# SBUF start addresses of matmul operands, first loads on a second queue, output pieces laid crosswise, row sums taken on VectorE

## The chip, the core and the metric

The kernel runs on one core of a Trainium2 chip. The number that counts is the time of one execution in device microseconds (us). Five engines work side by side, each on its own instructions in their order: TensorE (PE in the rows; its weight loads are PEld), VectorE (DVE), ScalarE (ACT), GpSimd (POOL) and SyncE (SP), which issues most of the DMAs. They wait for each other by semaphores.

## What is computed

One decoder layer over 256 tokens of width 1024, in float32, with five mixer branches that read the same input x. Cut to what matters:

```
h = x @ w_in + b_in                     # 1024 -> about 14000 columns: q, k, v, gates z, merge logits
o_a = causal attention                  # branch A
o_b = dilated mixture:                  # branch B: three (q, k) groups, one v
      parts = [band(q_i, k_i, v, window, dilation) for the 3 groups]
      num/den merged over the groups    # = one softmax over the three groups' logits
o_c, o_d, o_e = forgetting attention, gated delta rule, memory cross-attention
o = stack(o_a .. o_e) * silu(z)
y = sum_n sigmoid(merge_logits_n) * (o_n @ w_branch_n)
y = y @ w_out
out = layer_norm(alpha * x + y) * ln_g + ln_b
```

## The kernel before

**Matmuls.** Every float32 operand of a large matmul is split into a high part (`hi`) and the rest (`lo`), both stored in a 4-byte matmul format: ScalarE writes `hi` by a copy (L123), VectorE writes `lo = src - hi` (L124). A product then takes three matmuls, `hi*hi`, `hi*lo`, `lo*hi` (`mm3`, L128). So weights are loaded to `raw` (4 KB a partition), split into `hi` and `lo`, and used from there. x is split once, into `xhi` and `xlo`.

**Units.** The work on weights is a list of units in the order `ORDER`. A projection unit (`fm_unit`) has 1024 weight columns, which is 24 matmuls with the 256 columns of x moving and 128 weight columns stationary; in the rows it reads `mm<-xhi,hi`, `mm<-xlo,hi`, `mm<-xhi,lo` (moving operand first). A merge of a branch (`merge_branch`) has eight pairs: one such unit for the merge logits, then a unit of nine matmuls in which the gated branch output moves (`mm<-f,hi`, `mm<-f,lo`). There are 40 pairs. The memory's keys take three units with `big` (the normalised memory) moving. A token-major block (`tm_block`) has the weights moving and x stationary; the first block of all is one of these, on `wcs` (402 columns, 48 matmuls). The last stage is y @ w_out: 120 matmuls with weights moving (512 or 256 columns) and `f` stationary, in five pieces.

**Order.** Units come one after the other; between their chunks, `stepper` emits the next step of side streams (attention of branches a, b, c, the delta rule, the memory's layer norm, cross-attention). A timeline scheduler then orders instructions on each engine, apart from those that `keep` pins to the order of the program. Loads run up to four units ahead, in five `raw` buffers (`NRAW`): SP issues a load when VectorE has made the `lo` part of the unit that used the buffer.

**Placing.** Tiles of a partition lie behind each other in the order in which the pools were opened. By the built program `xhi` and `xlo` start at bytes 16512 and 24704 (both 128 past a multiple of 512), the five `raw`, four `hi` and four `lo` buffers from byte 62144 on in steps of 4096 (all 192 past one), the sixteen `f3` buffers, where gated outputs and y lie, from 115392 on in steps of 3072 (192 past one), the `big` buffers from 164544 on (192 past one). Chunks of a tile that a matmul takes are 512 or 1024 bytes apart, so each keeps its tile's remainder.

**Start.** x comes in five pieces, two of 128 KB and three of 256 KB, between the four loads of `wcs`, all from SP; the pieces of x lie in two `raw` buffers.

**Branch b.** `attend` (L752 to L790) handles two heads at a time (a pair, x = 0, 1), three pairs. Per head: logits with mask and row minimum on VectorE (L752), exponentials on ScalarE (L768) for three groups with `accum_out`, which adds the row sums; VectorE adds group 1, then group 2, to group 0 (L771), adds the three row sums (L775), takes the reciprocal and scales (L781). TensorE transposes the result (L787).

**Tail.** `finish` computes block t of 128 tokens piece by piece into PSUM tiles of two banks. Both halves of block 0 lie in one tile, both of block 1 in the other. Each piece is read by VectorE (L1071), which adds the residual; statistics, reciprocal root and two VectorE instructions per half (L1062, L1063) follow, then the store.

Of the kernel before, what the change touches and what calls it, by code (L numbers as in the profile page):

```python
# [9 lines left out]
F32 = mybir.dt.float32  # L10
# [5 lines left out]
P = 128  # L16
S = 256
# [58 lines left out]
@with_exitstack  # L76
def kernel(ctx: ExitStack, tc: tile.TileContext, T: dict, out: bass.AP):
    nc = tc.nc
    cpool = ctx.enter_context(tc.tile_pool(name="cpool", bufs=1))
    wpool = ctx.enter_context(tc.tile_pool(name="wpool", bufs=3))  # L80
    f3 = ctx.enter_context(tc.tile_pool(name="f3", bufs=16))
    big = ctx.enter_context(tc.tile_pool(name="big", bufs=2))
    sp = ctx.enter_context(tc.tile_pool(name="sp", bufs=4))
    ps = ctx.enter_context(tc.tile_pool(name="ps", bufs=2, space=bass.MemoryType.PSUM))
    dr = ctx.enter_context(tc.tile_pool(name="dr", bufs=1, space=bass.MemoryType.DRAM))
# [33 lines left out]
        return pst("av", shape, 1)  # L119


    def split(hi, lo, src):
        A_.activation(hi, src, AF.Copy)  # L123
        V_.tensor_tensor(lo, src, hi.bitcast(F32), op=ALU.subtract)  # L124

    def mm3(pt, lh, ll, rh, rl, first, last, pin=False):
# [10 lines left out]
    HR = (slice(0, 64), slice(64, 128))  # L137


    xhi, xlo = ct("xhi", (P, KD, S), F32R), ct("xlo", (P, KD, S), F32R)  # L140
    cst = ct("cst", (P, C_N))
    vb, vcb = ct("vb", (P, 2, BW)), ct("vcb", (P, BW + 18))
    bcol = ct("bcol", (P, T["bcol"].shape[1]))
# [19 lines left out]
    class Unit:  # L163
# [7 lines left out]
        def load(self):  # L171
            self.r = wpool.tile([P, 1024], F32, tag="raw", name=nm("raw"), bufs=NRAW)
            for i, p in enumerate(self.parts):
                if self.before is not None:
                    self.before[0](i, len(self.parts))
                nc.sync.dma_start(self.r[:, p], self.src[:, p])

        def split(self):
            self.h = wpool.tile([P, 1024], F32R, tag="hi", name=nm("hi"), bufs=NHI)
            self.l = wpool.tile([P, 1024], F32R, tag="lo", name=nm("lo"), bufs=NHI)  # L180
            for i, p in enumerate(self.parts):
                if self.before is not None:
                    self.before[1](i, len(self.parts))
                split(self.h[:, p], self.l[:, p], self.r[:, p])

    def need(name):
        while name is not None and name not in done:
# [88 lines left out]
    xraw = {}  # L276

    def load_x(i, j, n):
        if i % 2 == 0 and j == 0:
            xraw["t"] = wpool.tile([P, 4, S], F32, tag="raw", name=nm("raw"), bufs=NRAW)  # L280
        w = 2 // n
        o = 2 * i + w * j
        xraw[i, j] = xraw["t"][:, o % 4:o % 4 + w]
        nc.sync.dma_start(xraw[i, j], T["xT"][:, o:o + w])

    def split_x(i, j, n):
        w = 2 // n
        o = 2 * i + w * j
        split(xhi[:, o:o + w], xlo[:, o:o + w], xraw[i, j])

    def evac_c(p, t):
        if t == 0:
# [10 lines left out]
    def consts():  # L303
        for _ in range(CW):
            yield 1
        nc.sync.dma_start(vcb, T["vcb"].to_broadcast([P, BW + 18]))
        nc.sync.dma_start(bcol, T["bcol"])
        nc.sync.dma_start(cw, T["convw"])
        nc.sync.dma_start(adt, T["adt"].to_broadcast([P, 12]))
        nc.sync.dma_start(cst[:, :C_MA], T["cst"][:, :C_MA])  # L310
        flag("consts")


# [6 lines left out]
    def scalars():  # L320

        yield from wait("sc")
        nc.sync.dma_start(cst[:, C_MA:], T["cst"][:, C_MA:])
        nc.sync.dma_start(gnw, T["gnw"])
        nc.sync.dma_start(mgb, T["mgb"])
        nc.sync.dma_start(vb, T["vb"].to_broadcast([P, 2, BW]))

        V_.tensor_scalar(cwh, cw, 0.5, None, op0=ALU.mult)
        hb = bcol[:, 3 * len(FM):]
        V_.tensor_scalar(hb, hb, 0.5, None, op0=ALU.mult)  # L330
        for n, f in [("z" + i, 0.5) for i in BR] + list(QSCALE.items()):
            i = FM.index(n) * 3
            V_.tensor_scalar(bcol[:, i:i + 3], bcol[:, i:i + 3], f, None, op0=ALU.mult)
        flag("bias")
        yield
        a, lp = ct("a", (P, 2, 12)), ct("lp", (P, 2, 12))
        e, s1, s2, ea = ct("e", (P, 24)), ct("s1", (P, 24)), ct("s2", (P, 24)), ct("ea", (P, 6))
        for t in range(2):
            V_.tensor_scalar(a[:, t, 0:6], sc[:, t, 0:6], -1.0, None, op0=ALU.mult)
            V_.tensor_tensor(a[:, t, 6:12], sc[:, t, 6:12], adt[:, 6:12], op=ALU.add)  # L340
        af, lpf = a.rearrange("p t c -> p (t c)"), lp.rearrange("p t c -> p (t c)")
        V_.scalar_tensor_tensor(e, af, -1.0, af, op0=ALU.mult, op1=ALU.max)
        A_.activation(beta, sc[:, :, 12:18], AF.Exp, scale=-1.0)
        A_.activation(ea, adt[:, 0:6], AF.Exp)
        yield
        A_.activation(e, e, AF.Exp, scale=-1.0)
        V_.tensor_scalar(beta, beta, 1.0, None, op0=ALU.add)
        V_.reciprocal(beta, beta)
        V_.tensor_scalar(ea, ea, -1.0, None, op0=ALU.mult)
        yield  # L350
        V_.tensor_scalar(s1, e, 2.0, None, op0=ALU.add)
        V_.reciprocal(s1, s1)
        V_.tensor_tensor(s1, s1, e, op=ALU.mult)
        V_.tensor_tensor(s2, s1, s1, op=ALU.mult)
        V_.tensor_scalar(lpf, s2, 2.0 / 17, None, op0=ALU.mult)
        for n in (15, 13, 11, 9, 7, 5, 3):
            V_.scalar_tensor_tensor(lpf, lpf, 2.0 / n, s2, op0=ALU.add, op1=ALU.mult)
        V_.scalar_tensor_tensor(lpf, lpf, 2.0, s1, op0=ALU.add, op1=ALU.mult)
        V_.scalar_tensor_tensor(lpf, af, 0.0, lpf, op0=ALU.max, op1=ALU.add)
        yield  # L360

        for t in range(2):
            V_.tensor_scalar(fg[:, t, 0:6], lp[:, t, 0:6], -1.0, None, op0=ALU.mult)
            V_.tensor_tensor(lp[:, t, 6:12], lp[:, t, 6:12], ea, op=ALU.mult)
            V_.tensor_scalar(fg[:, t, 6:12], lp[:, t, 6:12], MAGIC, -MAGIC, op0=ALU.add, op1=ALU.add)
            V_.tensor_tensor(fg[:, t, 12:18], lp[:, t, 6:12], fg[:, t, 6:12], op=ALU.subtract)
        yield BURST

        lg = lgps()
        pt, p2 = lg[:, 0, :36].rearrange("p (t c) -> p t c", t=2), lg[0:18, 1, :S]  # L370
        keep(PE.matmul(pt[:, 0], K(C_TRI), fg[:, 0], start=True, stop=True))
        keep(PE.matmul(pt[:, 1], K(C_ONE), fg[:, 0], start=True, stop=False))
        keep(PE.matmul(pt[:, 1], K(C_TRI), fg[:, 1], start=False, stop=True))
        keep(PE.matmul(p2, fg[:, 0], K(C_TRI, 256), start=True, stop=False))
        keep(PE.matmul(p2[:, P:], fg[:, 1], K(C_TRI), start=False, stop=True))
        yield
        V_.tensor_scalar(ngt, pt, -1.0, None, op0=ALU.mult)
        grow = ct("grow", (18, S))
        V_.tensor_copy(grow, p2)
        R["gscr"] = dr.tile([18, S], F32, name="gscr")  # L380
        yield
        nc.sync.dma_start(R["gscr"], grow)
        flag("scalars")
# [340 lines left out]
    def attend(br, groups, vname, maskf, width):  # L724
# [5 lines left out]
        def pair(m):  # L730
# [33 lines left out]
            for g in range(ng):  # L764
                for x in range(2):
                    l = L[x][g]
                    for t, sl in SL:
                        A_.activation(l[:, sl], l[:, sl], AF.Exp, bias=mms[x][:, t:t + 1], scale=-1.0, accum_out=sm_[x][:, t, g:g + 1])  # L768
                    yield
                    if g:  # L770
                        V_.tensor_tensor(L[x][0], L[x][0], l, op=ALU.add)  # L771
            for x in range(2):
                rs = spt("rs", (P, 2), bufs=4)
                if ng > 1:
                    V_.tensor_reduce(rs, sm_[x], axis=AX.X, op=ALU.add)  # L775
                    V_.reciprocal(rs, rs)
                else:
                    V_.reciprocal(rs, sm_[x][:, :, 0])
                l = L[x][0]
                for t, sl in SL:  # L780
                    V_.tensor_scalar(l[:, sl], l[:, sl], rs[:, t:t + 1], None, op0=ALU.mult)  # L781
# [237 lines left out]
    def out_units():  # L1019
# [12 lines left out]

        def chunk(u, k, t):
            if k == 0 and t == 0:
                lgs = [lgps() for _ in range(2)]
                fin["p"] = [[lg[:, i] for i in range(2)] for lg in lgs]
                fin["p"][1].append(mmps((P, 512)))
                warm = spt("warm", (P, 1), bufs=1)
                A_.activation(warm, yhl[2][0][:, 1, 0:1].bitcast(F32), AF.Sqrt, scale=0.0, bias=0.0)
# [10 lines left out]
        def finish():  # L1050
# [3 lines left out]
            def norm(t):  # L1054
# [4 lines left out]
                V_.reciprocal(rs, rs)  # L1059
                for c, cs in enumerate((slice(0, 512), slice(512, 1024))):  # L1060
                    o = xres[:, t, cs]
                    V_.scalar_tensor_tensor(o, o, mv[:, t, 0:1], lngb[:, 0, cs], op0=ALU.subtract, op1=ALU.mult)  # L1062
                    V_.scalar_tensor_tensor(o, o, rs, lngb[:, 1, cs], op0=ALU.mult, op1=ALU.add)  # L1063
                    (nc.sync, nc.scalar)[c].dma_start(out[t * P:(t + 1) * P, cs], o)
# [148 lines left out]
```

## Time and profile before

| | |
|---|---|
| median of three runs | 467.25 us (467.22 to 468.22) |
| the profiled execution | 469.32 us, of which its program's span is 467.2 us |
| matmuls in the profile | 4039, TensorE busy 96% of the span |
| granted clock of TensorE | 0.994 of full speed |

Durations below come from the one profiled execution; times in rows count from the start of its span, and 2.1 us lie outside the span. A busy TensorE is no sign of its best pace: matmuls overlap, and what counts is the time from the start of one to the start of the next.

### The profile page before, as it was taken

How to read it: one execution, taken by the hardware profiler on the slowest of the kernel's cores; microseconds unless marked ns; L12 is line 12 of the kernel's file. 1: busy time of each engine (PE TensorE's matmuls, PEld its weight loads, DVE VectorE, ACT ScalarE, POOL GpSimd, SP SyncE). 2: the span in 40 equal slices, each digit the busy share in tenths (PEclk: the TensorE clock that was granted, in tenths of full speed). 3: DMA queues.
4: the chain of work that ended last, by engine and by line, in shares of the span. 5: the costliest groups of instructions: out<-in, count | busy, mean ns of one | idle time of the engine just before them, and what ended most of it. 6: DMA issues, size and time to landing. Idle time of an engine off the chain costs nothing. (4 is left out here: it accounts for less than half of the span.)

```text
span 467.2 us, 10262 instructions
## 1 busy us (share of the span) xinstructions
PE 449.9 (96%) x4039; PEld 425.0 (91%) x4039; DVE 328.1 (70%) x757; ACT 265.5 (57%) x520; POOL 30.6 (7%) x36
## 2 busy tenths in 40 slices
PE   6999999999999999999999989999989999999993
PEld 3999999999998999999999989988989999999963
DVE  4799998877797535564655689895676565587746
ACT  5466685765666644444434976694684654475600
POOL 0000020010000000000000112100022112200000
PEclk9899999999999999999999999999999999999999
DMA  7978577555445545566434165564765445678202
GB/s 253 380 246 255 164 225 252 159 178 173 125 130 160 152 125 172 176 202 183 125 109 126 60 176 182 173 193 152 250 201 184 145 150 148 190 234 278 91 0 90
DMA packets 35051, 81.38 MB, mean 174 GB/s; under 512 B 8970, under 2 KB 17468, under 8 KB 34876
## 3 DMA queue, kind: packets, MB, share of 16 engines
q1 hardware_dynamic: 34715, 80.22, 55.8%
q8 instruction: 31, 0.51, 0.4%
q10 hardware_dynamic: 288, 0.52, 0.3%
q14 instruction: 17, 0.13, 0.1%
HBM read 79.37 MB, written 1.36 MB: 173 GB/s over the span
## 5 line engine op out<-in xcount | busy, mean ns | idle before, releaser
L124 DVE TENSOR_TENSOR lo<-raw,hi 128x1024 fp32r<-128x1024 f32 (+4 forms) x163 | 169.3, 1040 | 83.4 <-ACT hi L123 80.8
L128 PE MATMUL mm<-xhi,hi 128*128 128x256 f32 x776 | 219.5, 283 | 1.2 <-DVE yt L993 1.2
L128 PE MATMUL mm<-xhi,lo 128*128 128x256 f32 x776 | 216.1, 279 | 1.3 <-DVE lo L124 1.3
L128 PE MATMUL mm<-xlo,hi 128*128 128x256 f32 x776 | 216.5, 279 | 0.0
L123 ACT ACTIVATE hi<-raw 128x1024 fp32r<-128x1024 f32 (+4 forms) x163 | 146.0, 899 | 111.9 <-PE mm L128 83.5
L128 PEld LDWEIGHTS mm<-xhi,hi 128*128 128x128 f32 x776 | 146.3, 189 | 5.8 <-issue 2.7
L128 PEld LDWEIGHTS mm<-xhi,lo 128*128 128x128 f32 x776 | 145.8, 188 | 1.8 <-DVE lo L124 1.7
L128 PEld LDWEIGHTS mm<-xlo,hi 128*128 128x128 f32 x776 | 146.0, 188 | 0.8 <-issue 0.8
L128 PE MATMUL mm<-f,hi 128*128 128x256 f32 x240 | 44.7, 282 | 0.7 <-ACT th L976 0.7
L994 POOL TENSOR_TENSOR yacc<-yacc,yt 128x256 f32<-128x256 f32 x24 | 24.4, 1018 | 280.0 <-DVE yt L993 275.2
L128 PEld LDWEIGHTS mm<-f,hi 128*128 128x128 f32 x240 | 36.6, 188 | 1.6 <-ACT th L976 1.3
L128 PE MATMUL mm<-f,lo 128*128 128x256 f32 x120 | 33.7, 281 | 0.0
L128 PEld LDWEIGHTS mm<-f,lo 128*128 128x128 f32 x120 | 22.6, 188 | 0.0
L128 PE MATMUL mm<-hi,xhi 128*128 128x384 f32 (+1 forms) x48 | 16.6, 363 | 2.1 <-ACT hi L123 2.1
L135 PE MATMUL lg<-f,f 64*128 64x256 f32 (+2 forms) x192 | 18.5, 354 | 0.0
L976 ACT ACTIVATE th<-mm,bcol 128x256 f32<-128x256 f32 x40 | 18.5, 462 | 0.0
L768 ACT ACTIVATE pr<-pr,mm 128x128 f32<-128x128 f32 (+1 forms) x36 | 15.9, 443 | 4.5 <-DVE mm L759 4.5
L128 PE MATMUL mm<-lo,xhi 128*128 128x384 f32 (+1 forms) x48 | 17.3, 360 | 0.4 <-DVE lo L124 0.4
L128 PE MATMUL mm<-hi,xlo 128*128 128x384 f32 (+1 forms) x48 | 17.0, 354 | 0.0
L123 ACT ACTIVATE f<-og 128x256 fp32r<-128x256 f32 x12 | 4.9, 416 | 19.3 <-DVE og L695 15.3
L705 ACT ACTIVATE f<-mm,bcol 128x256 f32<-128x256 f32 x33 | 15.1, 456 | 0.0
L135 PEld LDWEIGHTS lg<-f,f 64*128 64x128 f32 (+1 forms) x192 | 12.5, 186 | 2.6 <-issue 0.9
(221 smaller groups left out, 529.9 us busy)
## 6 DMA issues: line engine op xcount, KB each, us to landing
raw<-in_wf_dram SPq DMA_DIRECT2D x60, 512.0 KB, 4.3
raw<-in_wm_dram SPq DMA_DIRECT2D x40, 512.0 KB, 4.0
raw<-in_wb_dram SPq DMA_DIRECT2D x40, 192.0 KB, 2.5
raw<-in_wt_dram SPq DMA_DIRECT2D x12, 384.0 KB, 3.5
raw<-in_wo_dram SPq DMA_DIRECT2D x8, 512.0 KB, 4.1
gr<-gscr SPq DMA_DIRECT2D x12, 128.0 KB, 3.5
raw<-in_wcs_dram SPq DMA_DIRECT2D x3, 402.0 KB, 5.6
raw<-in_mem_dram SPq DMA_DIRECT2D x2, 512.0 KB, 4.8
```

The lines of the kernel that those rows point to most:

```text
L123: A_.activation(hi, src, AF.Copy)
L124: V_.tensor_tensor(lo, src, hi.bitcast(F32), op=ALU.subtract)
L128: ins = PE.matmul(pt, l, r, start=start, stop=stop)
L135: keep(PE.matmul(pt, l, r, start=start, stop=stop))
L705: A_.activation(R[name][:, m], p, AF.Identity, bias=b, scale=1.0 if scale is None else scale)
L768: A_.activation(l[:, sl], l[:, sl], AF.Exp, bias=mms[x][:, t:t + 1], scale=-1.0, accum_out=sm_[x][:, t, g:g + 1])
L976: A_.activation(th, p, AF.Tanh, bias=bcol[:, i:i + 1], scale=0.5)
L994: (V_ if last else G_).tensor_tensor(yacc[:, d], yacc[:, d], yt, op=ALU.add)
```

## The change

1. Pools are opened in another order, with two filler tiles of 64 and 448 bytes. By the built program `xhi` and `xlo` stay at 16512 and 24704; `raw`, `hi` and `lo` start at 32960 and stay 192 past a multiple of 512; `f3` starts at 86656 and `big` at 135808, both now 128 past one (192 before).
2. x is loaded to one `big` tile instead of two `raw` buffers, its first two pieces from ScalarE's queue. The first loads, splits and constants are pinned.
3. In branch b the exponentials have no `accum_out`; group 1 is added on GpSimd, and group 2 by a VectorE instruction that also gives the row sum.
4. In the tail the first piece of both token blocks lies in one PSUM tile and the second piece of both in the other; the second half of block 0 is normalised by ScalarE and GpSimd.

```diff
@@ tile_hybrid_trunk_kernel
-    cpool = ctx.enter_context(tc.tile_pool(name="cpool", bufs=1))
+    xpool = ctx.enter_context(tc.tile_pool(name="xpool", bufs=1))
+    padw = ctx.enter_context(tc.tile_pool(name="padw", bufs=1))
     wpool = ctx.enter_context(tc.tile_pool(name="wpool", bufs=3))
+    padf = ctx.enter_context(tc.tile_pool(name="padf", bufs=1))
     f3 = ctx.enter_context(tc.tile_pool(name="f3", bufs=16))
     big = ctx.enter_context(tc.tile_pool(name="big", bufs=2))
+    cpool = ctx.enter_context(tc.tile_pool(name="cpool", bufs=1))
...
-    xhi, xlo = ct("xhi", (P, KD, S), F32R), ct("xlo", (P, KD, S), F32R)
+    padw.tile([P, 16], F32, name="padw")
+    padf.tile([P, 112], F32, name="padf")
+    xhi, xlo = [xpool.tile([P, KD, S], F32R, name=n) for n in ("xhi", "xlo")]
@@ load_x
-        if i % 2 == 0 and j == 0:
-            xraw["t"] = wpool.tile([P, 4, S], F32, tag="raw", name=nm("raw"), bufs=NRAW)
+        if i == 0 and j == 0:
+            xraw["t"] = bigt([P, KD, S])
...
-        nc.sync.dma_start(xraw[i, j], T["xT"][:, o:o + w])
+        keep((nc.scalar if i == 0 else nc.sync).dma_start(xraw[i, j], T["xT"][:, o:o + w]))
@@ consts
-        nc.sync.dma_start(vcb, T["vcb"].to_broadcast([P, BW + 18]))
+        keep(nc.sync.dma_start(vcb, T["vcb"].to_broadcast([P, BW + 18])))
...
@@ attend
-                        A_.activation(l[:, sl], l[:, sl], AF.Exp, bias=mms[x][:, t:t + 1], scale=-1.0, accum_out=sm_[x][:, t, g:g + 1])
+                        A_.activation(l[:, sl], l[:, sl], AF.Exp, bias=mms[x][:, t:t + 1], scale=-1.0,
+                                      accum_out=sm_[x][:, t, 0:1] if ng == 1 else None)
                     yield
-                    if g:
-                        V_.tensor_tensor(L[x][0], L[x][0], l, op=ALU.add)
+                    if 0 < g < ng - 1:
+                        G_.tensor_tensor(L[x][0], L[x][0], l, op=ALU.add)
+                    elif g:
+                        for t, sl in SL:
+                            V_.tensor_tensor_reduce(l[:, sl], L[x][0][:, sl], l[:, sl], 1.0, 0.0, ALU.add, ALU.add, sm_[x][:, t, 0:1])
+                        L[x][0] = l
...
-                if ng > 1:
-                    V_.tensor_reduce(rs, sm_[x], axis=AX.X, op=ALU.add)
-                    V_.reciprocal(rs, rs)
-                else:
-                    V_.reciprocal(rs, sm_[x][:, :, 0])
+                V_.reciprocal(rs, sm_[x][:, :, 0])
@@ out_units
-                fin["p"] = [[lg[:, i] for i in range(2)] for lg in lgs]
+                fin["p"] = [[lg[:, t_] for lg in lgs] for t_ in range(2)]
@@ finish, norm
                     o = xres[:, t, cs]
+                    if t == 0 and c == 1:
+                        nmr = ct("nmr", (P, 1))
+                        V_.tensor_scalar(nmr, rs, mv[:, t, 0:1], -1.0, op0=ALU.mult, op1=ALU.mult)
+                        A_.activation(o, o, AF.Identity, scale=rs, bias=nmr)
+                        G_.tensor_tensor(o, o, lngb[:, 0, cs], op=ALU.mult)
+                        G_.tensor_tensor(o, o, lngb[:, 1, cs], op=ALU.add)
+                        nc.scalar.dma_start(out[t * P:(t + 1) * P, cs], o)
+                        continue
```

Three places show what the change makes of the engines' order. First SP's queue at the start of the program, before (`in_xT_dram` is x, `in_wcs_dram` the first block's weights, `in_wf_dram` the following units' weights, the rest constants):

```order
L284 DMA raw_105<-in_xT_dram 128x256
L176 DMA raw_104<-in_wcs_dram 128x402
L284 DMA raw_105<-in_xT_dram 128x256
L176 DMA raw_104<-in_wcs_dram 128x402
L284 DMA raw_105<-in_xT_dram 128x512
L176 DMA raw_110<-in_wcs_dram 128x804
L284 DMA raw_114<-in_xT_dram 128x512
L176 DMA raw_113<-in_wcs_dram 128x804
L284 DMA raw_114<-in_xT_dram 128x512
L306 DMA vcb<-in_vcb_dram 128x402
L176 DMA raw_117<-in_wcs_dram 128x804
L307 DMA bcol<-in_bcol_dram 128x100
```

and the same queue in the changed kernel (its first two pieces of x are the first two entries of ScalarE's queue, ahead of the table load):

```order
L185 DMA raw_115<-in_wcs_dram 128x402 x2
L295 DMA big_116<-in_xT_dram 128x512
L185 DMA raw_121<-in_wcs_dram 128x804
L295 DMA big_116<-in_xT_dram 128x512
L185 DMA raw_124<-in_wcs_dram 128x804
L295 DMA big_116<-in_xT_dram 128x512
L185 DMA raw_127<-in_wcs_dram 128x804
L185 DMA raw_130<-in_wf_dram 128x1024
L185 DMA raw_172<-in_wf_dram 128x1024
L185 DMA raw_192<-in_wf_dram 128x1024
L185 DMA raw_210<-in_wf_dram 128x1024
L317 DMA vcb<-in_vcb_dram 128x402
```

The last load of `wcs` now stands ahead of every constant, and four loads of the next units do too.

Second, VectorE in the softmax of branch b, the first pair, before (L771 adds groups, L775 sums the three row sums):

```order
L771 TENSOR_TENSOR pr_3369<-pr_3369,pr_3375 128x384
L771 TENSOR_TENSOR pr_3369<-pr_3369,pr_3534 128x384
L775 TENSOR_REDUCE rs_3688<-sm_3317 128x2
L776 RECIPROCAL rs_3688<-rs_3688 128x2
L781 TENSOR_SCALAR pr_3369<-pr_3369,rs_3688 128x128
L781 TENSOR_SCALAR pr_3369<-pr_3369,rs_3688 128x256
```

and in the changed kernel, where L787 adds group 2 and gives the row sum of both groups' sum, in two column ranges:

```order
L787 ISA pr_3544,sm_3327<-pr_3379,pr_3544 128x128
L787 ISA sm_3327 128x1
L787 ISA pr_3544,sm_3327<-pr_3379,pr_3544 128x256
L787 ISA sm_3327 128x1
L791 RECIPROCAL rs_3700<-sm_3327 128x2
L794 TENSOR_SCALAR pr_3544<-pr_3544,rs_3700 128x128
L794 TENSOR_SCALAR pr_3544<-pr_3544,rs_3700 128x256
```

The addition of group 1 has gone to GpSimd's queue, between its additions to `yacc`.

Third, VectorE in the tail, before (`lg_6041` is the PSUM tile of block 0, `lg_6042` that of block 1):

```order
L1071 SCALAR_TENSOR_TENSOR big_4561<-lg_6041,big_4561 128x512
L1072 BN_STATS st_6105<-big_4561 128x6
L1071 SCALAR_TENSOR_TENSOR big_4561<-lg_6041,big_4561 128x512
L1072 BN_STATS st_6105<-big_4561 128x6
L1055 BN_AGGR mv<-st_6105 128x2
L1057 TENSOR_SCALAR rstd<-mv 128x1
L1062 SCALAR_TENSOR_TENSOR big_4561<-big_4561,mv,big_4563 128x512 x2
L1059 RECIPROCAL rstd<-rstd 128x1
L1071 SCALAR_TENSOR_TENSOR big_4561<-lg_6042,big_4561 128x512
```

and in the changed kernel:

```order
L1094 SCALAR_TENSOR_TENSOR big_4571<-lg_6051,big_4571 128x512
L1095 BN_STATS st_6115<-big_4571 128x6
L1094 SCALAR_TENSOR_TENSOR big_4571<-lg_6052,big_4571 128x512
L1095 BN_STATS st_6115<-big_4571 128x6
L1069 BN_AGGR mv<-st_6115 128x2
L1071 TENSOR_SCALAR rstd<-mv 128x1
L1085 SCALAR_TENSOR_TENSOR big_4571<-big_4571,mv,big_4573 128x512
L1073 RECIPROCAL rstd<-rstd 128x1
L1086 SCALAR_TENSOR_TENSOR big_4571<-big_4571,rstd,big_4573 128x512
L1079 TENSOR_SCALAR nmr<-rstd,mv 128x1
L1094 SCALAR_TENSOR_TENSOR big_4571<-lg_6051,big_4571 128x512
```

The two pieces of block 0 are now read from different tiles, and one full-width instruction of each kind (L1062, L1063) has left the engine between them and block 1.

## Rows read from the trace of the kernel before

**Rows 1.** The chain that ended last, in order: start, length, engine, tile, line.
```profile
447.40 0.70 DVE big L1071
...
448.14 7.15 PE lg L128 x30
...
455.32 0.70 DVE big L1071
```

**Rows 2.** Who waited for whom: us in total, times, longest.
```profile
PEld lg L787 <- DVE pr L781: 0.4, 2, 0.3
```

**Rows 3.** Branch b's stretch: start:end, length, busy per engine, clock, DMA share, GB/s.
```profile
266.00:346.00 80.00, 75.41 (x606) 70.26 (x606) 64.09 (x161) 56.95 (x126) 7.87 (x8) 1.00 0.58 182
```

**Rows 4.** Timeline of TensorE, matmuls of an x unit, every seventh here.
```profile
39.80 0.28 PE L128 MATMUL mm<-xhi,hi 128*128 128x256 f32 x1
...
40.59 0.28 PE L128 MATMUL mm<-xlo,hi 128*128 128x256 f32 x1
```

**Rows 5.** The same after attention matmuls, nine matmuls apart.
```profile
164.87 0.28 PE L128 MATMUL mm<-xhi,hi 128*128 128x256 f32 x1
...
165.93 0.28 PE L128 MATMUL mm<-xhi,hi 128*128 128x256 f32 x1
```

**Rows 6.** A memory-key unit, nine matmuls apart.
```profile
314.82 0.28 PE L128 MATMUL mm<-big,lo 128*128 128x256 f32 x1
...
315.90 0.28 PE L128 MATMUL mm<-big,lo 128*128 128x256 f32 x1
```

**Rows 7.** One pair of the last merge: x unit, gated unit, next pair.
```profile
427.83 0.29 PE L128 MATMUL mm<-xhi,hi 128*128 128x256 f32 x1
...
430.57 0.39 PE L128 MATMUL mm<-f,hi 128*128 128x256 f32 x2
...
431.63 0.29 PE L128 MATMUL mm<-xhi,hi 128*128 128x256 f32 x1
```

**Rows 8.** Timeline of the start; in brackets idle time before, and releaser.
```profile
7.32 0.33 SPq L176 DMA_DIRECT2D raw<-in_wcs_dram  x1
...
9.70 0.63 PE L128 MATMUL mm<-hi,xhi 128*128 128x402 f32 x2 [1.37 <-ACT hi L123]
...
12.87 0.88 ACT L123 ACTIVATE hi<-raw 128x804 fp32r<-128x804 f32 x1 [0.85 <-DMA raw<-in_wcs_dram]
...
18.60 0.29 PE L128 MATMUL mm<-xhi,hi 128*128 128x256 f32 x1
```

**Rows 9.** A stretch of the start, columns as in rows 3.
```profile
11.00:14.60 3.60, 3.60 (x13) 3.56 (x13) 3.35 (x14) 2.07 (x4) 0.00 (x0) 0.53 1.05 332
```

**Rows 10.** Memory-key matmuls with the high part stationary: count, busy, mean ns, idle before.
```profile
L128 PE MATMUL mm<-big,hi 128*128 128x256 f32 x48 | 9.3, 291 | 0.7 <-ACT f L705 0.6
```

**Rows 11.** Groups of VectorE and ScalarE, 255 to 350 us, columns as in rows 10.
```profile
L771 DVE TENSOR_TENSOR pr<-pr,pr 128x384 f32<-128x384 f32 x12 | 6.6, 554 | 5.1 <-ACT pr L768 5.0
...
L752 DVE CUSTOM_DVE_ANT_0 pr<-lg,cst 128x256 f32<-128x256 f32 x14 | 5.8, 417 | 0.0
...
L752 DVE CUSTOM_DVE_ANT_0 pr<-lg,cst 128x128 f32<-128x128 f32 x14 | 4.0, 282 | 0.0
...
L752 DVE DVE_READ_ACCUMULATOR2_ANT mx<- 128x1 f32 x28 | 2.3, 81 | 0.0
...
L775 DVE TENSOR_REDUCE rs<-sm 128x2 f32<-128x6 f32 x6 | 0.9, 149 | 0.0
...
L768 ACT ACTIVATION_READ_ACCUMULATOR pr<-pr,mm 128x1 f32 x36 | 6.8, 188 | 0.0
```

**Rows 12.** GpSimd's additions, all of the span.
```profile
L994 POOL TENSOR_TENSOR yacc<-yacc,yt 128x256 f32<-128x256 f32 x24 | 24.4, 1018 | 280.0 <-DVE yt L993 275.2 <-DVE mm L759 4.8
```

**Rows 13.** VectorE's split of 1024 columns, beside a GpSimd addition and alone.
```profile
339.08 0.75 POOL L994 TENSOR_TENSOR yacc<-yacc,yt 128x256 f32<-128x256 f32 x1 [42.52 <-DVE yt L993]
...
339.48 1.44 DVE L124 TENSOR_TENSOR lo<-raw,hi 128x1024 fp32r<-128x1024 f32 x1 [0.47 <-ACT hi L123]
...
344.10 1.23 DVE L124 TENSOR_TENSOR lo<-raw,hi 128x1024 fp32r<-128x1024 f32 x1 [0.52 <-ACT hi L123]
```

More of the change, by code (lines that the diff above doesn't have):

```diff
@@ L119, in avps, with split @@
         return pst("av", shape, 1)
-    def split(hi, lo, src):
-        A_.activation(hi, src, AF.Copy)
+    def split(hi, lo, src, pin=False):
+        ins = A_.activation(hi, src, AF.Copy)
+        if pin:
+            keep(ins)
         V_.tensor_tensor(lo, src, hi.bitcast(F32), op=ALU.subtract)
@@ L175, in load @@
                     self.before[0](i, len(self.parts))
-                nc.sync.dma_start(self.r[:, p], self.src[:, p])
+                ins = nc.sync.dma_start(self.r[:, p], self.src[:, p])
+                if self.before is not None:
+                    keep(ins)
         def split(self):
@@ L183, in split @@
                     self.before[1](i, len(self.parts))
-                split(self.h[:, p], self.l[:, p], self.r[:, p])
+                split(self.h[:, p], self.l[:, p], self.r[:, p], self.before is not None)
     def need(name):
@@ L278, in load_x @@
     def load_x(i, j, n):
-        if i % 2 == 0 and j == 0:
-            xraw["t"] = wpool.tile([P, 4, S], F32, tag="raw", name=nm("raw"), bufs=NRAW)
+        if i == 0 and j == 0:
+            xraw["t"] = bigt([P, KD, S])
         w = 2 // n
         o = 2 * i + w * j
-        xraw[i, j] = xraw["t"][:, o % 4:o % 4 + w]
-        nc.sync.dma_start(xraw[i, j], T["xT"][:, o:o + w])
+        xraw[i, j] = xraw["t"][:, o:o + w]
+        keep((nc.scalar if i == 0 else nc.sync).dma_start(xraw[i, j], T["xT"][:, o:o + w]))
     def split_x(i, j, n):
@@ L288, in split_x @@
         o = 2 * i + w * j
-        split(xhi[:, o:o + w], xlo[:, o:o + w], xraw[i, j])
+        split(xhi[:, o:o + w], xlo[:, o:o + w], xraw[i, j], True)
     def evac_c(p, t):
@@ L305, in consts @@
             yield 1
-        nc.sync.dma_start(vcb, T["vcb"].to_broadcast([P, BW + 18]))
[L307 to L310, printed above, removed]
+        keep(nc.sync.dma_start(vcb, T["vcb"].to_broadcast([P, BW + 18])))
+        keep(nc.sync.dma_start(bcol, T["bcol"]))
+        keep(nc.sync.dma_start(cw, T["convw"]))
+        keep(nc.sync.dma_start(adt, T["adt"].to_broadcast([P, 12])))
+        keep(nc.sync.dma_start(cst[:, :C_MA], T["cst"][:, :C_MA]))
         flag("consts")
@@ L322, in scalars @@
         yield from wait("sc")
[L323 to L326, printed above, removed]
+        keep(nc.sync.dma_start(cst[:, C_MA:], T["cst"][:, C_MA:]))
+        keep(nc.sync.dma_start(gnw, T["gnw"]))
+        keep(nc.sync.dma_start(mgb, T["mgb"]))
+        keep(nc.sync.dma_start(vb, T["vb"].to_broadcast([P, 2, BW])))
         V_.tensor_scalar(cwh, cw, 0.5, None, op0=ALU.mult)
```

## The prediction

> **What bounds the kernel now.** [...] Between two stretches of matmuls stands a VectorE instruction of 0.70 us, and TensorE goes on only when it has ended: VectorE begins at 447.40 and TensorE's next matmul at 448.14 [rows 1]. VectorE is reading one half of a PSUM tile and the next matmuls write its other half. In the list of waits I looked for the places that the change touches besides, above all the transposes of branch b: they waited 0.4 us in all [rows 2]. So branch b's softmax hardly holds TensorE up directly. Yet over its whole stretch, 266 to 346 us, TensorE is busy 75.41 of 80 us, that is 4.59 us idle [rows 3].
>
> Then the pace inside the units, read as distance between starts. An undisturbed x unit makes seven matmuls in 0.79 us, 113 ns each [rows 4]. The same operands, after attention matmuls, make nine in 1.06 us, 118 ns each [rows 5], and in the units that I followed this lasted until something else interrupted them. So matmuls with x moving and weights stationary have two paces, and what came before picks one. The memory-key units make nine in 1.08 us, 120 ns [rows 6]. In a merge the x unit takes 430.57 − 427.83 = 2.74 us for 24 matmuls (114 ns; its first three are the late ones, the other 21 make 113 ns) and the gated unit 431.63 − 430.57 = 1.06 us for nine (118 ns) [rows 7]. A pair is 3.80 us.
>
> What differs between these by the stated placing: x at 128 past a multiple of 512 with weights at 192 can have the fast pace; `f3` and `big`, at 192 with weights at 192, show 118 to 120 ns. One trace with one placing can't tell whether the remainder is the cause.
>
> Last the start. The last load of `wcs` is issued only at 7.32 us, and ScalarE's last split of it starts at 12.87 after waiting for that load; TensorE waited 1.37 us ahead of 9.70 and reaches the first x unit at 18.60 [rows 8]. [...]
>
> **The tail.** The crosswise pieces take both waits away: while VectorE reads block 0's piece, TensorE writes block 1's into the other tile's bank. Each wait is 448.14 − 447.40 = 0.74 us, the second alike since its VectorE instruction has the same length [rows 1]: −1.48 us. It costs some moves: block 0's second half is scaled by ScalarE and two GpSimd instructions. I bound the latter by GpSimd's additions, 1.02 us for 256 columns [rows 12], so about 2 us each for 512, and 5 us for all. They start near 455 and end near 460, ahead of block 1's last normalisation, which lies behind the last matmul; ScalarE's queue holds that store's issue ahead of block 1's square root, so only a path more than some 2 us longer than I think would reach the end. The end after the last matmul is the same work as before: 0.
>
> **Pace in merges.** The gated units get `f3` at 128 against weights at 192, the pair of remainders that x has. So nine matmuls could go at 113 ns, 1.02 us, and the x unit behind them loses its three late ones: a pair of 33 matmuls would be 33 × 113.3 ns = 3.74 us, −0.06 us, and over 40 pairs −2.4 us. Here is a catch. Before, each x unit in the merge stretches stands on the fast pace right behind a gated unit; if the changed remainder also takes away what sets it there, all 33 can stand at 118 ns: 3.89 us, +0.09 us, +3.5 us over 40 pairs. Between these I take −1.2 us, half of the best, since attention leaves some units on the slow pace [rows 5] and the fast one is what undisturbed stretches show.
>
> [...]
>
> **Memory keys.** Three units of 24, of which the 48 with the high part stationary are one row [rows 10], so 72 matmuls go from 120 ns to 113 or 118: −0.5 to −0.1, I take −0.35 us. The output stage has its moving weights still at 192 and only the stationary `f` moved; its mirror, x stationary, shows me nothing better: 0.
>
> **Start.** Constants now stand behind `wcs`: `vcb` and `bcol`, 128 × 502 × 4 bytes = 257 KB, at the 332 GB/s of that time [rows 9] 0.77 us; and the last load no longer waits for a raw buffer at 7.32. I take 0.75 us earlier, and 0.35 for the clock, as the 3.6 us at 0.53 hold 1.7 us of lost time [rows 9], of which a fifth comes back if TensorE idles less. So −1.1 us; bounds 0 (the DMA engines are full anyway and the same bytes must land) and −2.9 (0.75, all of the 1.7, and some 0.4 of the 1.37 us wait). The pinned constants are needed when the first x units' results are read, at about 18; if they came late by more than the gain, the gain is gone, no more.
>
> **Branch b.** ScalarE loses 36 reads of an accumulator at 188 ns, 6.8 us. VectorE loses twelve additions, 6.6 us, and six small sums, 0.9 us; it gains six joint additions, each in two parts that I price by the nearest such form with a reduction, 417 + 282 + 2 × 81 = 861 ns, 5.2 us [rows 11]. Net −2.3 us. GpSimd gains six additions of 384 columns: between 0.75 × 1.5 = 1.13 us and 1.02 × 1.5 = 1.53 us each [rows 12, 13]. What comes of it on TensorE is at most the idle 4.59 us of the stretch; the streams wait for many things there, and I take −1.0 us. Bounds −4.6 and, by the last rival, +5.9.
>
> A VectorE split beside a GpSimd addition took 1.44 us, alone 1.23 [rows 13]. Six additions would so cost VectorE 6 × 0.21 = 1.3 us, which lowers its net relief of 2.3 to about 1.0. [...]
>
> **Sum.** −1.5 −1.2 −0.35 −1.1 −1.0 = −5.15 us. The profiled execution took 469.32 (span 467.2 and 2.1 outside), the median is 467.25; I take the same 5.15 from the median: **462.1 us**.
>
> **Rivals.** *Only the tail counts* (0.13): the distance between starts has nothing to do with the remainder, the start is bound by the DMA engines, branch b lies beside other work. For it: the share of 1.05 and the 0.4 us at the transposes; against: no other difference that I see between the 113 and 120 ns rows. 467.25 − 1.5 = 465.8 us.
>
> *The fast pace is lost in the merges* (0.10): x and gated units at the same remainders stay where attention left them, at 118 ns: +3.5 in place of −1.2, 462.1 + 4.7 = 466.8 us. For it: [rows 5]; against: [rows 4], where a long run stays fast.
>
> *GpSimd in the softmax of branch b* (0.07; the one that ends slower): the addition of group 1 stands on GpSimd between additions to `yacc`, and the exponentials' chain of each head waits for it. It takes up to 1.53 us where VectorE took 0.55, 0.98 more six times, 5.9 us if all of it reaches the transposes, and no gain in b: 462.1 + 1.0 + 5.9 = 469.0 us. Against: those waited only 0.4 us. It decides once these waits exceed the other gains, 4.15 us.
>
> **Chances and range.** The forecast holds 0.70. 0.2% of the time, about 0.9 us, is what a measurement can tell from no change. The forecast and the first rival are faster: 0.83; the second lies within 0.9 us of 467.25: 0.10; the last is slower: 0.07. The range takes in the forecast's own terms and the first rival and leaves out the other two, 0.17. Below, the merges at their best (−1.2 more) with the start at its best (−1.8 more) give 459.1; allowing branch b some of its idle time besides, 458.5. Above, 465.8 and what lies around it: 466.2.
>
> **What would show it.** Right: no wait of TensorE behind the VectorE reads of the tail; nine gated matmuls in about 1.02 us and memory keys at 113 to 118 ns; the first x unit near 17.5 us; idle time of TensorE in branch b's stretch below 4.59. Wrong: x units behind gated units at 118 ns, transposes of branch b that wait for VectorE or GpSimd for microseconds, VectorE splits stretched beside GpSimd more than 0.2 us, waits for constants ahead of 20 us, or a store of block 0's second half that ends after block 1's.

## The result, and the profile after

The changed kernel takes 462.36 us in the median of four runs (460.9 to 463.02), the kernel before 467.74 us in the median of four (467.22 to 469.27): ratio 0.985, interval 0.9825 to 0.9879, so faster, by less than 2%. The forecast was 462.1. The two medians by themselves give 0.9885, just outside that interval: three of the four runs of the kernel before are those of the table ahead of the change, and the fourth took 469.27. Beside the later runs the kernel before took 468.8 to 469.5 us in the median, so the gain is nearer to 7 us than to the 5.4 of these medians. Its profiled execution has a span of 460.2 us against 467.2, so these two executions lie 7.0 us apart where the medians lie 5.4 apart.

The chain that ended last shows the tail:

```profile
385.63 45.10 PE mm L135 x396
...
438.95 12.13 PE lg L135 x60
451.08 1.79 PE mm L135 x15
```

The 60 matmuls that stood in three parts with a VectorE instruction between them [rows 1] are one piece now. The 396 matmuls ahead of the output stage are the last twelve pairs, that is the last merge and the second half of the one before; they take 45.10 us. From TensorE's timeline the first x unit, then a pair from the first half of the merge before the last one, and a pair of the last merge:

```profile
15.97 0.29 PE L135 MATMUL mm<-xhi,hi 128*128 128x256 f32 x1
...
379.07 0.40 PE L135 MATMUL mm<-f,hi 128*128 128x256 f32 x2
...
380.13 0.28 PE L135 MATMUL mm<-xhi,hi 128*128 128x256 f32 x1
...
382.96 0.40 PE L135 MATMUL mm<-f,hi 128*128 128x256 f32 x2
...
425.81 0.28 PE L135 MATMUL mm<-f,hi 128*128 128x256 f32 x1
...
426.83 0.28 PE L135 MATMUL mm<-xhi,hi 128*128 128x256 f32 x1
...
429.55 0.28 PE L135 MATMUL mm<-f,hi 128*128 128x256 f32 x1
```

The later pair, one of these twelve, is what the prediction hoped for: a gated unit in 1.02 us (1.06 in [rows 7]), an x unit in 2.72 (2.74). The other is what its second rival feared: 1.06 and 2.83 us, all 33 matmuls at 118 ns. The slow pace holds from 341 to 347 and from 355 to 384 us, and earlier around 250 and 270 us; the fast one holds through the last twelve pairs. Of the 40 gated units 30 stand at 113 to 116 ns and 10 at 118.

Branch b's stretch and the end of it, columns as in [rows 3], and two rows of the wait list:

```profile
266.00:346.00 80.00, 77.84 (x628) 73.40 (x627) 62.44 (x161) 54.84 (x101) 13.18 (x12) 0.98 0.62 196
...
332.00:341.00 9.00, 7.03 (x47) 6.64 (x46) 6.10 (x18) 6.10 (x9) 1.96 (x2) 0.81 0.66 216
```

```profile
DVE pr L787 <- POOL pr L784: 5.5, 3, 3.2
...
PE mm L135 <- ACT th L989: 1.8, 1, 1.8
```

The first x unit starts 2.63 us earlier than in [rows 8]. TensorE idles 2.16 us in branch b's stretch, not 4.59 [rows 3]. In branch b's last pair VectorE waits 3.2 us for GpSimd. TensorE waits 1.8 us for the sigmoid L989, where the kernel before had one such wait of 0.7 us. ScalarE's timeline shows the sigmoid behind that pair's twelve exponentials, with a split and a copy of x between:

```profile
327.55 4.27 ACT L779 ACTIVATE pr<-pr,mm 128x128 f32<-128x128 f32 x12 [1.80 <-DVE mm L770]
...
333.62 0.45 ACT L989 ACTIVATE th<-mm,bcol 128x256 f32<-128x256 f32 x1
```

Behind this wait the granted clock falls: it is 1.00 until 335 us, 0.50 from 336 to 338, and 0.81 on average from 332 to 341 us. Before 266 us the gain of the profiled execution is 2.0 us; it is 6.6 at 329, 4.2 behind the wait, 4.7 behind the low clock, 4.8 at the last x unit, and the tail adds 2.07.

### The profile page after: what moved, and what is told of

Its sections match the earlier page's. It is cut to its first block, busy times and chain, and to the rows that moved or that the text cites. A ratio compares the mean times of both kernels' runs of the same rounds, so it can differ in the third digit from the quotient of the medians.

```text
span 460.2 us, 10250 instructions
## 1 busy us (share of the span) xinstructions
PE 447.5 (97%) x4039; PEld 424.1 (92%) x4039; DVE 325.3 (71%) x762; ACT 263.1 (57%) x485; POOL 41.2 (9%) x44
## 4 chain that ended last, share of the span: by engine, by line
PE 94%; DVE 2%; DMA 1%; ACT 1%; issue 1%; SPq 0%; POOL 0%; DVEq 0%; ACTq 0%
PE mm L135 77%; PE lg L142 4%; PE lg L135 4%; PE av L142 2%; PE lg L800 1%; DMA raw<-in_wcs_dram 1%; PE lg L653 1%; DVE pr L787 0%; ACT hi L128 0%; PE lg L875 0%; PE lg L943 0%; PE lg L647 0%; PE lg L450 0%; ACT pr L779 0%; PE lg L669 0%
## 5 line engine op out<-in xcount | busy, mean ns | idle before, releaser
L131 DVE TENSOR_TENSOR lo<-raw,hi 128x1024 fp32r<-128x1024 f32 (+4 forms) x163 | 167.1, 1026 | 84.4 <-ACT hi L128 82.5
L135 PE MATMUL mm<-f,hi 128*128 128x256 f32 x240 | 43.7, 280 | 1.8 <-ACT th L989 1.8
L989 ACT ACTIVATE th<-mm,bcol 128x256 f32<-128x256 f32 x40 | 18.4, 460 | 0.1
L763 DVE CUSTOM_DVE_ANT_0 pr<-lg,cst 128x128 f32<-128x128 f32 (+1 forms) x48 | 14.1, 349 | 1.0 <-PE lg L142 1.0
L499 POOL TENSOR_SCALAR_AFFINE_SELECT pr<-pr 128x256 f32<-128x256 f32 x6 | 6.3, 1063 | 94.3 <-DVE pr L498 76.3
```

What stands on the lines that cost most here:

```text
L135: ins = PE.matmul(pt, l, r, start=start, stop=stop)
L499: G_.affine_select(E[:, 0::2], E[:, 0::2], pattern=[[0, 2], [1, P]], compare_op=ALU.is_ge, fill=-BIG, base=0, channel_multiplier=-1)
L763: V_.tensor_tensor_reduce(l[:, sl], pts[x][:, sl], mk[x][:, sl], 1.0, 3.0e38, ALU.add, ALU.min, mx[x][:, t, g:g + 1])
L989: A_.activation(th, p, AF.Tanh, bias=bcol[:, i:i + 1], scale=0.5)
```

## Experiments

**Each part alone.** Four runs each took one part of the change into the kernel before.

```diff
@@ tail alone: as in the change, with the new tile among the constants
+                        nmr = ct("nmr", (P, 1))
...
@@ placing alone
+    padw.tile([P, 16], F32, name="padw")
+    padf.tile([P, 112], F32, name="padf")
...
@@ start alone
+            xraw["t"] = bigt([P, KD, S])
...
+        keep((nc.scalar if i == 0 else nc.sync).dma_start(xraw[i, j], T["xT"][:, o:o + w]))
@@ row sums alone
+                        G_.tensor_tensor(L[x][0], L[x][0], l, op=ALU.add)
...
+                            V_.tensor_tensor_reduce(l[:, sl], L[x][0][:, sl], l[:, sl], 1.0, 0.0, ALU.add, ALU.add, sm_[x][:, t, 0:1])
```

> The kernel before with the tail's part alone (crosswise pieces, block 0's second half on ScalarE and GpSimd). My theory: both waits of TensorE on the VectorE reads go, 1.48 us, and nothing else moves: faster by 1.3 to 1.7 us. Rival, GpSimd's path of block 0 is the new end: within 0.5 us of before.

> The kernel before with the new placing alone (gated outputs and big 128 instead of 192 past a multiple of 512). My theory: the remainder sets whether a matmul can reach 113 ns: gated units at 113 or 118 and never 120, memory keys the same, output stage 0.5 us shorter, but no unit puts the x units back on the fast pace any more; in all between -2.5 and +1 us. Rival, the remainder means nothing: gated units at 118 to 120 ns as before, memory keys at 120, time within 0.5 us.

> The kernel before with the start's part alone (x into one big tile, first pieces from ScalarE's queue, pinned loads). My theory: the first x unit starts near 16.0 instead of 18.6 us and the granted clock stays at its upper level, of which the program keeps 1 to 2.6 us. Rival, the pinned constants come late: the gain is used up by waits before 60 us, within 0.5 us of before.

> The kernel before with branch b's row sums alone (no accumulating exponentials, group 1 added on GpSimd, joint addition and sum on VectorE). My theory: branch b's stretch gets shorter by 2 to 4.5 us up to the last pair and gives back some 2 us in a wait for GpSimd's additions in the last pair: faster by 1.5 to 3 us. Rival, the stretch is bound by the order of units and TensorE's pace there: within 0.5 us.

Ratios to the kernel before: tail 1.0095 (1.0065 to 1.0124), placing 0.9993 (0.9972 to 1.0013), start 0.9979 (0.996 to 0.9999), row sums 0.9916 (0.9893 to 0.9939). The row sums brought 3.9 us, more than the 1.5 to 3 expected.

The tail alone was slower, which neither theory had. Its chain names the place (the tail's matmuls are its second row):

```profile
392.94 47.24 PE mm L128 x396
...
448.52 12.02 PE lg L128 x60
```

In the kernel before, the same places and the two other parts of the 60 matmuls read:

```profile
389.80 45.80 PE mm L128 x396
...
443.93 3.44 PE lg L128 x15
...
456.06 2.06 PE lg L128 x15
```

The tail is mended as expected, but the twelve pairs ahead of it take 47.24 us instead of 45.80, and the merges before them lost as well. The new tile of 4 bytes (32 in the placing) stood ahead of weights, gated outputs and big, and moved them all from 192 to 224 past a multiple of 512; x stayed at 128. All 97 x units of that run stand at 117 to 119 ns, and none at 113. So the remainder moved the time in a run that was not meant to try it. The same part was run once more with that tile behind the big buffers.

```diff
-                        nmr = ct("nmr", (P, 1))
+                        nmr = spt("nmr", (P, 1), bufs=1)
```

> The tail's part alone once more, with the small new tile behind the big buffers, so that no other tile moves (in the first tail run it stood ahead of them and moved weights, gated outputs and big from 192 to 224 past a multiple of 512). My theory: the 32 bytes made that run slow, so x and gated units are back at 114 to 118 ns and both waits of the tail go: faster by 1 to 2 us. Rival, the tail's own work costs the program: slower by 1 to 4 us as in that run.

Ratio 0.996 (0.9938 to 0.9982), and

```profile
390.41 45.80 PE mm L128 x396
...
444.55 12.02 PE lg L128 x60
```

The pairs are back at 45.80 us; 32 bytes were worth 1.3% of the kernel. From the last gated unit to the last fifteen of these 60 matmuls it is 2.06 us less than before, more than the two waits' 1.48: in the chain of the kernel before the three parts of 15, 30 and 15 matmuls (the lines above and [rows 1]) took 3.44, 7.15 and 2.06 us, 12.65 in all, against 12.02 here, so by this difference each restart behind a wait had cost some 0.3 us too (an estimate from these rows).

Placing alone: the last twelve pairs took

```profile
389.44 46.84 PE mm L133 x396
```

that is 118.3 ns each, all on the slow pace, where the changed kernel has 45.10 us. Other pairs of the same run stood at 113: 21 of its 40 gated units are slow. It gains and loses, and its ratio cannot be told from 1.

Start alone: first x unit at 16.36 us. But the kernel's profiled executions without this part (before, and five of the runs told here) have it at 18.60, 17.33, 16.81, 18.48, 16.99 and 16.72, the six with it between 15.97 and 16.52. In 7 to 17 us the mean granted clock was 0.83 in the two latest of these and 1.00 in the other four: the low clock of [rows 9] is not in every execution. So the mean gain is 1.2 us (17.49 less 16.30), not the 2.6 of two traces. The first twelve x units of the changed kernel then stand at 118 ns and give 0.8 us of it back; so do those of the other five executions with this part, but eleven or more do so too in both runs on the tail, which don't have it.

**The whole change, with one thing undone.** First the placing of gated outputs and big, then GpSimd's addition, then both; every engine's order of the first is that of the changed kernel.

```diff
@@ b2_after_f192, c3_dve_f192
-    padf.tile([P, 112], F32, name="padf")
+    padf.tile([P, 128], F32, name="padf")
@@ b3_after_dve, c3_dve_f192
-                        G_.tensor_tensor(L[x][0], L[x][0], l, op=ALU.add)
+                        V_.tensor_tensor(L[x][0], L[x][0], l, op=ALU.add)
```

> The changed kernel with 64 more filler bytes, so that gated outputs and big are 192 past a multiple of 512 again; every engine's order is the same. My theory: gated units at 118 to 120 ns, memory keys at 120, first matmuls of the output stage at 230 to 235 ns, but every x unit behind a gated unit on the fast pace: between -0.5 and +2 us against the changed kernel. Rival, the remainder means nothing: within 0.5 us and no pace differs.

> The changed kernel with the addition of group 1 on VectorE instead of GpSimd. My theory: the wait for GpSimd in the last pair of branch b, 3.2 us of VectorE, goes, and with it the 1.8 us wait of TensorE and the stretch at its lower clock behind it: faster than the changed kernel by 1 to 2.5 us. Rival, VectorE's six more additions of 0.55 us, 3.3 us, hold up its splits: the same time or slower.

> The changed kernel unchanged, beside the others on one chip. My theory: the paces follow from program and placing, so the x units between 355 and 384 us stand at 118 ns again and the last merge at 113. Rival, they are drawn anew in each execution: another pattern.

> The changed kernel with gated outputs and big at 192 again and group 1 added on VectorE. My theory: its wait in the last pair and the slow x units behind gated units both go: faster than the changed kernel by 0.5 to 1.5 us. Rival, both are worth nothing once the order changes: within 0.5 us of it.

Ratios to the kernel before: placing undone 0.9868 (0.9834 to 0.9901), GpSimd's addition undone 0.9852 (0.9822 to 0.9882), the changed kernel again 0.9832 (0.9799 to 0.9864), both undone 0.986 (0.9834 to 0.9885). All intervals overlap. With gated outputs at 192 the last twelve pairs are back at 45.80 us, 0.70 more than changed, and the first merge takes 0.4 us more; the six pairs before the last twelve, on the slow pace in the changed kernel, are 0.4 us shorter. What this part of the change is worth can't be told from nothing by these times. Neither can the cost of GpSimd's addition. With it undone VectorE does not wait for GpSimd, but TensorE waits the same 1.8 us for L989: that wait is not GpSimd's, and my expectation fell. The run on row sums alone has 1.7 us of it. No version beats the changed kernel; the one with both undone stood at 462.05 us beside its 460.74.

The changed kernel's second profile shows the same pace in most units, and in every one from 340 us on, as expected. But five of the 97 x units (four of them from 107 to 121 us) and two of the 40 gated units stand at 118 ns where they stood at 113. So program and placing set most of the pattern and not all of it. What differed besides was the clock behind the wait in the last pair:

```profile
332.00:341.00 9.00, 7.05 (x59) 6.66 (x58) 7.43 (x21) 7.61 (x13) 2.07 (x3) 1.00 0.68 219
```

1.00 here, 0.81 above, after an equal wait. From the x unit right behind the wait to the next one it takes 1.5 us less than in the first profile; this goes with the drop and not with the change.

**What pays in branch b.** The row sums' part with ScalarE's accumulators put back.

```diff
-                                      accum_out=sm_[x][:, t, 0:1] if ng == 1 else None)
+                                      accum_out=sm_[x][:, t, g:g + 1])
```

> The run on branch b's row sums once more, with ScalarE's exponentials accumulating again (36 reads of 188 ns, 6.8 us, their results unused): group 1 still added on GpSimd, joint addition and sum still on VectorE. My theory: what pays is ScalarE's relief in the chain from logits to transposes, so most of the 4 us gained there goes: 0 to -1.5 us against the kernel before. Rival, VectorE's relief pays: as fast as that run, -3 to -4.5 us.

Ratio 0.9967 (0.9943 to 0.9991), against 0.9916 without them: about 1.5 us of 3.9 remain, so by the times more than half hangs on ScalarE's 36 reads; the two runs stood on different chips, and their intervals nearly touch. The two profiles put less on it: from x unit 63 to x unit 76 the kernel before took 79.3 us, this run 2.24 us less, the row sums alone 3.19 less. VectorE's groups in the run on row sums alone:

```profile
L776 DVE CUSTOM_DVE_ANT_0 pr<-pr,pr 128x128 f32<-128x128 f32 x6 | 3.3, 548 | 5.5 <-POOL pr L773 5.5
L776 DVE CUSTOM_DVE_ANT_0 pr<-pr,pr 128x256 f32<-128x256 f32 x6 | 2.5, 418 | 0.0
```

The mean of 548 ns mixes two durations. From the timeline of the changed kernel, the same instruction with no addition of GpSimd beside it, then GpSimd's second addition of the last pair and the instruction beside it:

```profile
258.08 0.29 DVE L787 CUSTOM_DVE_ANT_0 pr<-pr,pr 128x128 f32<-128x128 f32 x1 [0.98 <-POOL pr L784]
...
330.80 1.02 POOL L784 TENSOR_TENSOR pr<-pr,pr 128x384 f32<-128x384 f32 x1
...
330.87 1.09 DVE L787 CUSTOM_DVE_ANT_0 pr<-pr,pr 128x128 f32<-128x128 f32 x1 [3.23 <-POOL pr L784]
```

Four of the six take 0.25 to 0.29 us. The other two, in the second and the third pair, begin 0.07 us behind the start of GpSimd's addition and take 1.08 and 1.09 us, to 0.15 us behind its end.

**Pace by itself.** Two programs that compute no layer, only matmuls of 256 columns with 128 stationary ones in the kernel's pattern. In the first both operands lie at each of eight remainders of 512 (in the names a is 0, b 64, c 128, d 192 and so on; the moving operand first).

```diff
+    for rw in REM:
+        for rx in REM:
+            for half in range(2):
+                for b in range(1 + half):
+                    keep(nc.tensor.matmul(brk[:, :P], raw[:64, b, :P], raw[:64, b, P:], start=True, stop=True))
+                for i in range(8):
...
+                    for n, (w, x) in enumerate(((wh, xh), (wh, xl), (wl, xh))):
+                        keep(nc.tensor.matmul(mm, w[:, k], x[:, k], start=i + n == 0, stop=i == 7 and n == 2))
```

> No layer is computed: only matmuls of 256 columns in the kernel's pattern of three, with moving and stationary operands at 8 remainders each of 512 bytes, 24 matmuls behind a break of one and again behind one of two float32 matmuls. My theory: moving 128 with stationary 192 shows 113 or 118 ns, both at 192 show 120, and the pace goes by the two remainders' difference and not by either alone. Rival, one pace for all, within 2 ns.

Four of the 64 pairs, each shown by two matmuls 15 apart:

```profile
209.42 0.28 PE L61 MATMUL mm<-xha,whd 128*128 128x256 f32 x1
...
211.19 0.28 PE L61 MATMUL mm<-xha,whd 128*128 128x256 f32 x1
...
216.51 0.29 PE L61 MATMUL mm<-xhb,whd 128*128 128x256 f32 x1
...
218.29 0.28 PE L61 MATMUL mm<-xhb,whd 128*128 128x256 f32 x1
...
227.19 0.28 PE L61 MATMUL mm<-xhc,whd 128*128 128x256 f32 x1
...
228.89 0.28 PE L61 MATMUL mm<-xhc,whd 128*128 128x256 f32 x1
...
230.56 0.28 PE L61 MATMUL mm<-xhd,whd 128*128 128x256 f32 x1
...
232.36 0.28 PE L61 MATMUL mm<-xhd,whd 128*128 128x256 f32 x1
```

1.77, 1.78, 1.70 and 1.80 us for 15: 118.0, 118.7, 113.3 and 120.0 ns, with moving at 0, 64, 128, 192 and stationary at 192. The whole table goes by one number, stationary minus moving remainder, modulo 256: 0 gives 120.0, 64 gives 113.3, 128 gives 118.7, 192 gives 117.8, within 0.5 ns behind either break. Differences that are no multiple of 64, like the 96 of the first tail run, are not in it. So at 192 and 128 the kernel has the best of the four for its x units. The four differ by 6%, and what makes them differ no run here shows.

The slow pace of x units in the kernel is not in this table, so the second program took the pair 128 and 192 alone, behind breaks of several kinds.

```diff
+    for rows in (64, 128):
+        for cols in (32, 64, 96, 128):
+            for count in (1, 2, 3, 6, 8):
+                f32(rows, cols, count)
+                unit(128, 192)
```

> No layer is computed: only 24 matmuls each with moving 128 and stationary 192, behind breaks of float32 matmuls of several sizes and counts, behind waits for ScalarE, and between short units at other remainders. My theory: the break sets a phase between the two operands, so some breaks leave 118 ns for all 24 and units at 192 and 192 bring 113 back. Rival, 113 ns behind every break, and the 118 ns of the kernel come from work of other engines.

```profile
88.11 1.13 PE L60 MATMUL brk<-raw 64*128 64x96 f32 x8
...
91.10 0.28 PE L56 MATMUL mm<-xhc,whd 128*128 128x256 f32 x1
...
92.12 0.28 PE L56 MATMUL mm<-xhc,whd 128*128 128x256 f32 x1
...
120.40 0.53 PE L60 MATMUL brk<-raw 128*128 128x32 f32 x4
...
121.20 0.28 PE L56 MATMUL mm<-xhc,whd 128*128 128x256 f32 x1
...
122.26 0.28 PE L56 MATMUL mm<-xhc,whd 128*128 128x256 f32 x1
```

Nine matmuls in 1.02 us behind the first break, in 1.06 behind the second. Behind all 20 breaks on 64 rows the unit stands at 113 ns; behind 10 of the 20 on all 128 rows at 118 for its 24 matmuls, in a stretch where the program issues matmuls alone. So in this run a break on 128 rows moved units from one pace to the other, both ways, and the pace then stayed for the unit. A break on 64 rows seems to leave it as it was: all but the first of those 20 stood behind fast units, and further on two units behind such a break and a slow unit (at 312.03 and 324.24 us) are slow too. Short units with moving at 64 (difference 128) put the next unit on 118 and 113 in turn. Short units at 192 and 192 always left 113 behind, but they began behind fast units, so that they cure a slow one is shown only by the kernel before (an x unit at 118 ns from 191.08 us, a gated unit at 194.01, the x unit from 195.08 at 113). The writes by ScalarE did not make TensorE wait, so breaks by waiting were not tried.

## Why the prediction was right, point by point

- **Tail, −1.5:** right in place and kind. Alone it measured 0.996 or −1.9 us, in the traces −2.06; the step left out the slow restart behind each wait. GpSimd's two instructions took 1.29 us each where I wrote 2.
- **Pace in merges, −1.2, and memory keys, −0.35:** mis-sized. The dependence on the remainders holds (in the program of matmuls difference 64 gives 113 ns, 0 gives 120), but so does its catch. In the changed kernel 10 of the 40 gated units stand at 118 ns, in the placing alone 21; by the prediction's own prices for a pair that is an estimated 30 × −0.06 + 10 × 0.09 = −0.9 us and +0.8 us. The memory keys stand at 118, 118 and 114 ns. The runs can't tell the two terms from nothing, neither by the placing alone (0.9993) nor by its undoing. The failed step is "I take −1.2 us, half of the best": a pair on the slow pace loses more than one on the fast pace gains, and I set no weight on how many pairs stand on which.
- **Start, −1.1:** 0.9979, or −1.0 us. The working behind it was weaker than its result: the low clock of [rows 9] stands in two of the six executions without this part. That a fifth of the lost time comes back if TensorE idles less, the 0.35 us of the term, was an estimate that no run shows; what the runs show is that behind an equal wait of 1.8 us the clock fell in one execution of the changed kernel and stayed at 1.00 in the other.
- **Branch b, −1.0:** mis-sized; −3.9 us alone (0.9916). In the run on row sums alone 2.40 us of idle time are left in the window of [rows 3] where 4.59 were, and its units 63 to 76 took 3.19 us less. I took the transposes' 0.4 us of waits [rows 2] for a sign that the chain hardly holds TensorE, while the gain came in the units around them, through ScalarE's queue and, since 2.24 us remained with ScalarE's reads put back, probably VectorE's. How much of ScalarE's 6.8 us reached them is open, 2.4 us by the times and 0.95 by the profiles. VectorE's joint pair is as priced, 0.29 + 0.42 + 2 × 0.08 = 0.87 us where I had 0.861, when GpSimd is idle; twice it took 0.8 us more beside GpSimd's addition. So the 0.21 us from [rows 13] was no price for an addition: when the split there began, 0.35 of the addition's 0.75 us were left, and 0.21 of these were lost. In that split and in the last pair VectorE lost all but some 0.15 us of what was left of GpSimd's addition, 0.35 us and 0.95. GpSimd's addition took 1.01 us where I had 1.13 to 1.53.
- **Sum:** −5.15 forecast, −5.4 measured by the medians, some −7 by the ratio, and −8.1 in the repeat (460.74 beside 468.81). The four parts alone add up to −1.9 − 0.3 − 1.0 − 3.9 = −7.1 us, and their ratios multiplied give 0.985, that of the whole. So two errors of opposite sign cancel in part: branch b brought 2.9 us more and the tail 0.4, the placing 1.3 less. That the time still came out at 462.36 beside the 462.1 forecast is partly luck: the forecast counts from 467.25, the median of three runs, and beside the later runs the kernel before stood 1.6 to 2.2 us higher.
- **Rivals:** "only the tail counts" is out by the row sums' run. The lost pace is real in 10 of the 40 pairs. GpSimd in the softmax: VectorE waits 5.5 us for it, and the time without it can't be told from the time with it. The held-up VectorE doesn't set TensorE's wait there, which is for ScalarE's sigmoid.

What stays open: what the new placing is worth by itself, why the profiles put 0.95 us on ScalarE's accumulators and the times about 2.4, and what in a break on 128 rows sets the pace.

## What to carry to other kernels

Before comparing two versions, look where every operand of the large matmuls starts: a new 4-byte tile cost 1.3% here and hid a gain of 0.4%. Take pace from starts nine or more apart, in several places, since one operand pair ran at two paces here, 113 and 118 ns. Of a start-up time (the first x unit stood between 16.72 and 18.60 us without the new start) or a clock drop (0.81 and 1.00 over the same stretch), look at several executions before giving it a price; and run each part of a change alone, since a right sum can hide two wrong terms.

## What the runs showed of the hardware that I had not expected

In the first program of matmuls alone the pace went by stationary minus moving start address modulo 256 bytes, tried in steps of 64: 113.3 to 120.0 ns for 256 columns. At difference 64 the second program and the kernels showed two paces, 113.3 and 117.8 ns. In the second program the work before a unit went with its pace (113 ns behind all 20 breaks on 64 rows, 118 behind 10 of the 20 on 128), which lasted for its 24 matmuls; in the changed kernel two executions had each pace in nearly the same units. A VectorE addition of the changed kernel that began 0.07 us behind the start of a GpSimd addition took 1.09 us, where 0.29 was its time with none beside it. After an equal wait of 1.8 us the granted clock of the changed kernel fell in one execution (0.81 from 332 to 341 us) and stayed at 1.00 in the other.
